# Two transformer blocks on one core: the second block's adaLN weight pieces loaded from the last gate projection to the seventh output block

## Chip, cores and metric

One core of one Trainium2 chip. The metric is device microseconds (us) of one execution of the program. The profiled execution is one of these; its span runs from the first to the last instruction of the program. Engines: PE multiplies matrices, DVE and ACT are the vector and scalar engines, POOL is GpSimd, SP issues nearly all loads.

## What is computed

A first block (retention and mLSTM mixer, then a gated feed-forward) and behind it a second block with two layers (attention mixers, each with an expert-choice feed-forward), on 256 tokens of width 1024. Cut to what the change touches:

```
# first block, end: output projection of the mixer, then the feed-forward (hidden width 2816)
x = x + g1 * mixer_output(...)
x = x + g2 * swiglu(modulate(rms_norm(x, norm2_gain[layer]), sh2, sc2), w_ffn_in[layer], w_ffn_out[layer])
# second block: six modulation vectors for each layer and each of two streams
m_lat = jnp.split((silu_c @ mod_w[layer] + mod_b[layer])[:, None, :], 6, axis=-1)
m_ctx = jnp.split((silu_cc @ mod_w[layer] + mod_b[layer])[:, None, :], 6, axis=-1)
h_lat = rms_norm_2(x_lat, norm1_g[layer]) * (1 + m_lat[1]) + m_lat[0]
```

All is in float32. The adaLN weights `mod_w` are 1024 x 6144 for each of two layers. They depend on nothing of the first block, so they can be multiplied whenever there is room.

## The kernel before

**Weights come as pieces through a ring.** Every weight matrix is cut into pieces of up to 2 MB (128 partitions x 4096 columns). `pieces` is one long list (lines 218 to 228) that says in which order they are loaded. Three buffers, R0, R1 and R2, take them in turn; other buffers (F, G, L, H, Y) join in where they are free. `Ring.done(slot)` says that a piece has been used; the next piece of the list is then loaded into that slot by a transfer that SP issues, and SP waits for the slot's last reader first. SP works through its instructions in order, so a transfer that waits holds those behind it.

**The names of the pieces.** `wout0` and `wout1` are the mixer's output projection, `fin0` to `fin10` the eleven column blocks of the feed-forward's first matrix, `fout0` to `fout7` the eight pieces of its second. The adaLN weights of the second block are 24 pieces, `moda0` to `moda11` (layer 0) and `modb0` to `modb11` (layer 1). In the trace and the order all tiles of the ring are called R, and the weights are `w_out`, `w_fin`, `w_fout`, `mod0` and `mod1`.

**How a weight block is multiplied.** `prod` takes cuts of 4 rows of 128 x 256 columns. Each cut is split into a high part (ACT, line 303) and the remainder (DVE, line 304), and each product is made of three matmuls (high x high, high x low, low x high). The splits go to three pairs of buffers (w4k twice, w4p once), so they run up to three cuts ahead of PE. A block `fin` is 4 cuts of 24 matmuls, 96 in all; a pair of `fout` pieces is 6 cuts and 132 matmuls. A ring slot is free as soon as its last cut is split.

**How an adaLN piece is multiplied.** Unsplit: `mod_group` (line 374) takes four pieces into one accumulator; each piece is 8 matmuls of 32x512, which the trace shows as 16 instructions on tile `aux`. After the fourth, ACT or DVE copies the sums out (`ev`), and four small matmuls (`aux<-cp,ev`, 8 instructions in the trace) put them in place. Six groups make the 24 pieces.

**What sets the place of a piece.** `aside` registers a generator, and `tick`, called after each job of `prod`, moves every generator one step. A step of `mod_group` is taken only if its piece is in the ring's list of loaded pieces. `need` ticks until a piece is there; `drain` ticks until the generators are done. So the code is written in an order that follows the list of pieces; a scheduler then orders each engine's instructions, and each engine runs them in that order.

```
    mods = [f"moda{i}" for i in range(12)] + [f"modb{i}" for i in range(12)]
    for i in range(11):
        seq(f"fin{i}", mods[3 + i])
    for i in range(8):
        seq(f"fout{i}", mods[14 + i])
    seq("evkv0", *mods[22:], "evin0", "evin1", "evin2", "evout0", "evout1")
```

Before, the list has one piece beside each `fin` and each `fout` block and the last two behind `evkv0`, the first weights of the second block. The groups are registered after the mixer's output projection (line 1037), between it and the norm that makes the feed-forward's input (`norm_sums`, L2 of the residual, then tile L).

Of the kernel before, what the change touches and what calls it, by code (L numbers as in the profile page):

```python
# [91 lines left out]
def body(ctx, tc, T, dbg=None, stop_at=None):  # L92
# [71 lines left out]
    def aside(*gens):  # L164
        g = chain(gens)
        beside.append(g)
        return g
# [5 lines left out]
    def after(g):  # L173
        while g in beside:
            yield
# [6 lines left out]
    def drain(upto=None):  # L182
        while beside and (upto is None or upto in beside):
            tick()
# [24 lines left out]
    def seq(*names):  # L209
        for n in names:  # L210
            base = n.rstrip("0123456789")
            src, cols = SRC[base]
            one(base, T[src], int(n[len(base):]), cols)
# [5 lines left out]
           "odukv": ("od_ukv", 2048), "oduq": ("od_uq", 2304), "odout": ("od_out", SLOT)}  # L219
    seq("ada0", "ada2", "win0", "ada1", "ada3", "win1", "ada4", "win2", "ada5", "win3", "ada6", "win4", "ada7",  # L220
        "win5", "ada8", "win6", "ada9", "win8", "win9", "win7", "win10", "ada10", "win11", "ada11", "up0", "up1",
        "wout0", "moda0", "wout1", "moda1", "moda2")
    mods = [f"moda{i}" for i in range(12)] + [f"modb{i}" for i in range(12)]
    for i in range(11):
        seq(f"fin{i}", mods[3 + i])
    for i in range(8):
        seq(f"fout{i}", mods[14 + i])
    seq("evkv0", *mods[22:], "evin0", "evin1", "evin2", "evout0", "evout1")

    def expert_pieces(layer):  # L230
        def add(e, *ws):
# [14 lines left out]
    ring = Ring(nc, slot, pieces)  # L246
# [6 lines left out]
    def S(name):  # L253
        a, b = off[name]
        return sm[:, a:b]
# [120 lines left out]
    def mod_group(names, bias, MOD):  # L376


        i0 = 4 * int(names[0][4:])
        ps = None  # L380
        for j, name in enumerate(names):
            while not ring.has(name):
                yield
            s_, W = ring.get(name)
            Wv = kv3(W)
            ps = aux() if ps is None else ps
            for k in range(2):
                for q in range(4):
                    mm(ps[32 * q:32 * q + 32, :], sT2[:, 2 * q + k, 6 - 2 * j:38 - 2 * j], Wv[:, 2 * q + k, :],
                       start=j == 0 and k == 0, stop=j == 3 and k == 1, tile_position=(0, 32 * q), skip_group_check=True)  # L390
            ring.done(s_)
            yield
        ev = work("ev", 512, 1)
        evac(ev, ps)
        yield
        p2 = aux()
        for c in range(4):
            mm(p2[:, 8 * c:8 * c + 8], ev[:, c * 128:c * 128 + 128], selm)
        dve.tensor_tensor(MOD[:, i0:i0 + 16, :].rearrange("p (i c) r -> p i c r", c=4),
                          p2[:, :32].rearrange("p (c i r) -> p i c r", c=4, i=4),  # L400
                          bias[:, i0:i0 + 16].rearrange("p (i c) -> p i c", c=4)[:, :, :, None].to_broadcast([P, 4, 4, 2]),
                          op=OP.add)

    def groups(*which):

        return aside(*[mod_group([f"mod{'ab'[g // 3]}{g % 3 * 4 + j}" for j in range(4)],
                                 S(f"mod_b{g // 3}"), (MOD20, MOD21)[g // 3]) for g in which])

    def need(name):

# [4 lines left out]
    def mod_steps0(name, sT, bias, MOD):  # L415

        i = int(name[4:] if name.startswith("mod") else name[3:])
        while not ring.has(name):
            yield
        s_, W = ring.get(name)  # L420
        Wv = kv3(W)
        ev = work("ev", 512, 1)
        for k in range(KC):
            sk = sT[:, k, 0:1]
            if k == 0:
                dve.tensor_scalar_mul(ev, Wv[:, k, :], sk)
            else:
                dve.scalar_tensor_tensor(ev, Wv[:, k, :], sk, ev, op0=OP.mult, op1=OP.add)
            if k % 2:
                yield  # L430
        ring.done(s_)
        p2 = aux()
        for c in range(4):
            mm(p2[:, c:c + 1], ev[:, c * 128:c * 128 + 128], ones[:, 0:1])
        dve.tensor_tensor(MOD[:, i * 4:i * 4 + 4, 0], p2[:, :4], bias[:, i * 4:i * 4 + 4], op=OP.add)
# [533 lines left out]
    for t in range(2):  # L969
        r = head_rstd(MLN[:, t, :], "hm", 512)  # L970
        m3 = MLN[:, t, :].rearrange("p (h c) -> p h c", h=4)
        dve.tensor_tensor(m3, m3, r[:, :4, None].to_broadcast([P, 4, 128]), op=OP.mult)
    aside(*[mod_steps0(f"ada{i}", sT1, S("b_ada"), MOD1) for i in (10, 11)])
    bg_proj(3, "win11")
    ring.add("L")
    ring.retire("L")
# [38 lines left out]

    def out_proj(name, X2, X, gate, post):
        for i in range(2):
            s_, W = ring.get(f"{name}{i}")
            for n2 in range(2):
                ps = acc()  # L1020
                prod([kv3(W)[:, :, n2 * 256:n2 * 256 + 256]], [col(ps[:, :N], 0, X2, True), col(ps[:, N:], 1, X2)])
                k = i * 4 + 2 * n2
                for j in range(2):
                    residual(X, k + j, ps[:, j * N:j * N + N], gate(k + j))
                post(X, k)
            ring.done(s_)

    drain()
    g1h = cst.tile([P, KC], F32, name="g1h")
    dve.tensor_scalar_mul(g1h, MOD1[:, 16:24, 0], 0.5)  # L1030
    add, read = sums()
# [2 lines left out]
    A2x = scale_vec("A2x", MOD1, 4, 0, S("norm2"))  # L1034
    H2 = slot("L")
    H2h, H2l = xv(H2), xv(H2[:, 2048:])
    groups_ = groups(*range(6))
    norm_sums(XLv, read, A2x, MOD1[:, 24:32, 0], H2h, H2l)
    close_phase()
    wk[2] = ctx.enter_context(tc.tile_pool(name="late", bufs=1))  # L1040
# [992 lines left out]
```

## Time and profile before

| | us |
|---|---|
| median of 3 runs | 1914.63 (1913.92 to 1922.8) |
| the profiled execution | 1914.88 |
| its span | 1913.0 |
| PE busy | 1662.7 (87%) |
| DVE busy | 738.2 (39%) |
| ACT busy | 529.0 (28%) |
| HBM read | 579.59 MB |

How to read it: the span holds stages with different bounds. Up to about 780 us the first block and the second block's first mixer are multiplied; from about 820 on the experts' weights stream in. An engine's busy share says little by itself; what counts is where PE or the loads wait, and for what. Engine rows of a timeline give start and length in us, and in brackets the idle time before them with what ended it. The clock column is the share of PE's full clock (2.4 GHz) that was granted; its low level is half (1.2 GHz).

### The profile page before, as it was taken

How to read it: one execution, taken by the hardware profiler on the slowest of the kernel's cores; microseconds unless marked ns; L12 is line 12 of the kernel's file. 1: busy time of each engine (PE TensorE's matmuls, PEld its weight loads, DVE VectorE, ACT ScalarE, POOL GpSimd, SP SyncE). 2: the span in 40 equal slices, each digit the busy share in tenths (PEclk: the TensorE clock that was granted, in tenths of full speed). 3: DMA queues.
4: the chain of work that ended last, by engine and by line, in shares of the span. 5: the costliest groups of instructions: out<-in, count | busy, mean ns of one | idle time of the engine just before them, and what ended most of it. 6: DMA issues, size and time to landing. Idle time of an engine off the chain costs nothing. (4 is left out here: it accounts for less than half of the span.)

```text
span 1913.0 us, 29571 instructions
## 1 busy us (share of the span) xinstructions
PE 1662.7 (87%) x12876; PEld 1153.6 (60%) x12876; DVE 738.2 (39%) x1430; ACT 529.0 (28%) x916; POOL 52.7 (3%) x51
## 2 busy tenths in 40 slices
PE   7999999999999998799999989889997666575655
PEld 3999997889887778744343423258686323242323
DVE  5956786444536645611211212145763110010101
ACT  3423554434435553311010100034542100010000
POOL 0100021000000000000000000001000000000000
PEclk8999999999999999899999999999998877897888
DMA  9445457877784111589999999953356999999997
GB/s 379 185 182 220 160 194 267 336 296 315 286 310 167 66 61 74 233 345 428 428 430 428 428 428 429 428 226 121 133 220 266 426 427 426 427 427 426 426 426 302
DMA packets 53985, 582.54 MB, mean 305 GB/s; under 512 B 5984, under 2 KB 5984, under 8 KB 20576
## 3 DMA queue, kind: packets, MB, share of 16 engines
q1 hardware_dynamic: 53136, 577.90, 74.0%
q10 hardware_dynamic: 720, 2.75, 0.4%
q8 instruction: 101, 1.65, 0.3%
q14 instruction: 28, 0.23, 0.0%
HBM read 579.59 MB, written 1.05 MB: 304 GB/s over the span
## 5 line engine op out<-in xcount | busy, mean ns | idle before, releaser
L187 PE MATMUL acc<-L,w4k 128*128 128x256 f32 (+3 forms) x1744 | 269.3, 328 | 12.6 <-DMA L<-w 9.5
L187 PE MATMUL acc<-H,w4k 128*128 128x256 f32 (+2 forms) x1608 | 246.2, 338 | 18.1 <-DMA H<-w 11.6
L187 PEld LDWEIGHTS acc<-L,w4k 128*128 128x128 f32 (+2 forms) x1744 | 207.1, 178 | 53.0 <-issue 32.4
L304 DVE TENSOR_TENSOR w4k<-R,w4k 128x1024 fp32r<-128x1024 f32 (+3 forms) x152 | 177.7, 1170 | 137.3 <-ACT w4k L303 133.2
L187 PEld LDWEIGHTS acc<-H,w4k 128*128 128x128 f32 (+2 forms) x1608 | 189.2, 178 | 56.4 <-issue 30.2
L303 ACT ACTIVATE w4k<-R 128x1024 fp32r<-128x1024 f32 (+3 forms) x152 | 154.2, 1016 | 213.3 <-PE acc L187 189.6
L187 PE MATMUL acc<-R,w4k 128*32 128x256 f32 (+1 forms) x1136 | 157.4, 513 | 45.6 <-DMA R<-w 45.6
L187 PEld LDWEIGHTS acc<-R,w4k 128*32 128x32 f32 (+1 forms) x1136 | 55.7, 132 | 131.9 <-issue 65.1
L199 DVE COPY t2k<-acc 128x512 f32<-128x512 f32 x24 | 16.6, 692 | 271.6 <-PE acc L187 271.5
L187 PE MATMUL aux<-R,t2k 128*32 128x256 f32 (+3 forms) x656 | 87.8, 512 | 20.7 <-DMA R<-w 20.3
L187 PE MATMUL acc<-G,w4k 128*32 128x256 f32 (+1 forms) x622 | 87.5, 408 | 20.6 <-DMA G<-w 20.6
L197 ACT ACTIVATE w4p<-aux 32x512 f32<-32x512 f32 (+1 forms) x58 | 28.1, 485 | 253.0 <-PE aux L187 185.3
L199 DVE COPY w4p<-aux 32x512 f32<-32x512 f32 (+1 forms) x58 | 32.5, 560 | 155.0 <-ACT w4p L197 108.9
L187 PE MATMUL acc<-F,w4k 128*32 128x256 f32 (+2 forms) x464 | 74.5, 450 | 8.3 <-DMA F<-w 8.3
L187 PEld LDWEIGHTS acc<-G,w4k 128*32 128x32 f32 (+1 forms) x622 | 57.8, 166 | 37.6 <-DMA G<-w 26.4
L304 DVE TENSOR_TENSOR w4p<-R,w4p 128x1024 fp32r<-128x1024 f32 x43 | 54.3, 1262 | 56.7 <-ACT w4p L303 56.5
L190 PE MATMUL tr<-cp,t2k 128*128 128x128 f32 (+1 forms) x290 | 45.7, 284 | 33.8 <-DVE t2k L199 12.0
L197 ACT ACTIVATE t2k<-acc 128x512 f32<-128x512 f32 x24 | 14.3, 597 | 217.3 <-PE acc L187 217.3
L190 PEld LDWEIGHTS tr<-cp,t2k 128*128 128x128 f32 (+1 forms) x290 | 31.7, 143 | 70.1 <-issue 25.1
L187 PEld LDWEIGHTS aux<-R,t2k 128*32 128x32 f32 (+1 forms) x656 | 33.4, 137 | 65.0 <-issue 34.3
L187 PE MATMUL acc<-Y,w4k 128*32 128x256 f32 (+1 forms) x464 | 56.7, 477 | 16.5 <-DMA Y<-w 16.5
L303 ACT ACTIVATE w4p<-R 128x1024 fp32r<-128x1024 f32 x43 | 45.6, 1060 | 75.3 <-PE acc L187 61.2
(460 smaller groups left out, 2537.8 us busy)
## 6 DMA issues: line engine op xcount, KB each, us to landing
R<-w SPq DMA_DIRECT2D x67, 2048.0 KB, 28.3
R<-mod SPq DMA_DIRECT2D x24, 2048.0 KB, 8.5
F<-w SPq DMA_DIRECT2D x23, 2048.0 KB, 29.4
H<-w SPq DMA_DIRECT2D x23, 2048.0 KB, 29.2
L<-w SPq DMA_DIRECT2D x23, 2048.0 KB, 26.2
Y<-w SPq DMA_DIRECT2D x23, 2048.0 KB, 27.5
R<-w_in SPq DMA_DIRECT2D x11, 2048.0 KB, 7.9
R<-w_fin SPq DMA_DIRECT2D x10, 2048.0 KB, 9.6
```

The costliest lines, as they stand in the source:

```text
L187: return pe.matmul(out, lhsT, rhs, start=start, stop=stop, **kw)
L190: return pe.transpose(out, in_, ident[:in_.shape[0], :in_.shape[0]])
L197: act.activation(out, in_, AF.Copy, scale=1.0 if scale is None else scale)
L199: dve.tensor_copy(out, in_)
L303: act.activation(rnd(hi), src, AF.Copy)
L304: dve.tensor_tensor(rnd(lo), src, hi, op=OP.subtract)
```

## The change

The list of pieces is dealt out anew and the groups are registered earlier. `moda0` to `moda3` come among `wout0`, `wout1` and `fin0`; behind each of `fin1` to `fin10` follow one or two pieces (two behind `fin2`, `fin5` and `fin8`), behind `fout0` to `fout6` one each, and none behind `fout7` and `evkv0`. The six groups are registered before the last gate projection (`win11`), to begin when the first block's own last adaLN pieces (`ada10`, `ada11`) are through. `out_proj` gets its weights by `need` in place of `ring.get`, and the `drain` ahead of it waits for `ada_` alone.

```
-        "wout0", "moda0", "wout1", "moda1", "moda2")
+        "moda0", "wout0", "moda1", "wout1", "moda2", "fin0", "moda3")
     mods = [f"moda{i}" for i in range(12)] + [f"modb{i}" for i in range(12)]
-    for i in range(11):
-        seq(f"fin{i}", mods[3 + i])
+    mods = mods[:3:-1]
+    for i in range(1, 11):
+        seq(f"fin{i}", *[mods.pop() for j in range(1 + (i % 3 == 2))])
     for i in range(8):
-        seq(f"fout{i}", mods[14 + i])
-    seq("evkv0", *mods[22:], "evin0", "evin1", "evin2", "evout0", "evout1")
+        seq(f"fout{i}", *[mods.pop() for j in range(min(len(mods), 1))])
+    seq("evkv0", "evin0", "evin1", "evin2", "evout0", "evout1")
...
-    def groups(*which):
+    def group(g):
 
-        return aside(*[mod_group([f"mod{'ab'[g // 3]}{g % 3 * 4 + j}" for j in range(4)],
-                                 S(f"mod_b{g // 3}"), (MOD20, MOD21)[g // 3]) for g in which])
+        return mod_group([f"mod{'ab'[g // 3]}{g % 3 * 4 + j}" for j in range(4)], S(f"mod_b{g // 3}"), (MOD20, MOD21)[g // 3])
...
-    aside(*[mod_steps0(f"ada{i}", sT1, S("b_ada"), MOD1) for i in (10, 11)])
+    ada_ = aside(*[mod_steps0(f"ada{i}", sT1, S("b_ada"), MOD1) for i in (10, 11)])
+    groups_ = aside(after(ada_), *[group(g) for g in range(6)])
     bg_proj(3, "win11")
...
-            s_, W = ring.get(f"{name}{i}")
+            s_, W = need(f"{name}{i}")
...
-    drain()
+    drain(ada_)
...
-    groups_ = groups(*range(6))
     norm_sums(XLv, read, A2x, MOD1[:, 24:32, 0], H2h, H2l)
```

What this does to the order, at three places. In the rows, R0 to R2 are the ring's slots with a running number, `w4k` and `w4p` the split weights, `acc` and `aux` accumulators; a wait on PE is one for matmuls, on DVE for a split or a sum, on Activation for ACT's, on DMAHW for a landing.

**First place: SP's transfers around fin3.** Before, from `moda4`'s (R0_11) to `fin4`'s (R2_13):

```order
L69 DMA R0_11_3538<-mod0 128x4096 [waits DMAHW7_49,DMAHW2_49,PE_49]
L69 DMA R1_11_3639<-mod0 128x4096 [waits DMAHW4_49,DMAHW5_49,DMAHW3_49,DVE_49]
L69 DMA R0_12_3585<-w_fin 128x4096 [waits DMAHW2_49,PE_49]
L69 DMA R2_12_3777<-mod0 128x4096 [waits DMAHW0_49,DVE_49]
L69 DMA R1_12_3667<-w_fin 128x4096 [waits DMAHW3_49,PE_49]
L69 DMA R0_13_3915<-mod0 128x4096 [waits DMAHW4_49,DVE_49]
L69 DMA R2_13_3805<-w_fin 128x4096 [waits DMAHW5_49,PE_49]
```

and of the change, from `moda5`'s (R2_12) to `fin5`'s (R0_13):

```order
L69 DMA R2_12_3639<-mod0 128x4096 [waits DMAHW6_49,DMAHW5_49,DMAHW7_49,DMAHW0_49,DVE_49]
L69 DMA R1_12_3787<-mod0 128x4096 [waits DMAHW1_49,DVE_49]
L69 DMA R2_13_3667<-mod0 128x4096 [waits DMAHW4_49,PE_49]
L69 DMA R0_12_3933<-mod0 128x4096 [waits DMAHW2_49,DVE_49]
L69 DMA R2_14_3689<-w_fin 128x4096 [waits DMAHW6_49,PE_49]
L69 DMA R1_13_3815<-w_fin 128x4096 [waits DMAHW5_49,PE_49]
L69 DMA R0_13_3962<-w_fin 128x4096 [waits DMAHW7_49,PE_49]
```

Before, each slot carries one piece between two blocks (`fin3`, R1_12, follows R1_11). Now slot R2 carries two pieces in a row, `moda5` (R2_12) and `moda6` (R2_13), before `fin3` (R2_14), whose transfer waits for the matmuls of `moda6`. The same stands ahead of `fin6` (`moda9`, `moda10`) and `fin9` (`modb1`, `modb2`).

PE of the change there, from `moda6` to the first matmuls of `fin3` (acc_50 and acc_51); between the row of acc_48 and that of `ev_14` are 19 more matmuls of `fin2`:

```order
L187 MATMUL aux_33_3520<-R2_13_3667,sT2_112 32x512 [waits DMAHW6_49]
L187 MATMUL aux_33_3520<-R2_13_3667,sT2_112 32x512 x7
L187 MATMUL aux_33_3520<-R1_12_3787,sT2_112 32x512 [waits DMAHW5_49]
L187 MATMUL aux_33_3520<-R1_12_3787,sT2_112 32x512 x7
L187 MATMUL acc_48_3789<-L_3_3443,w4p_51_3893 128x256
...
L187 MATMUL aux_34_3847<-cp_68,ev_14_3829 128x8 [waits DMAHW1_49,DMAHW0_49,DVE_49]
L187 MATMUL aux_34_3847<-cp_68,ev_14_3829 128x8 x3
L187 MATMUL aux_35_3953<-R0_12_3933,sT2_112 32x512 [waits DMAHW7_49,PE_49]
L187 MATMUL aux_35_3953<-R0_12_3933,sT2_112 32x512 x7
L187 MATMUL acc_50_3935<-L_3_3443,w4k_105_3937 128x256 [waits Activation_49]
L187 MATMUL acc_51_3936<-L_3_3443,w4k_105_3937 128x256 [waits DVE_49]
L187 MATMUL acc_50_3935<-L_3_3443,w4k_106_3938 128x256 [waits DVE_49]
```

Before, 145 matmuls of blocks and one more piece stand between the matmuls of R1_11 and the first of `fin3`; now it is `moda7`, 20 matmuls, the small group and `moda8`.

**Second place: PE between the output projection and fin0.** Before (`tr_29` are the norm's sums, `tr_30` its broadcast, acc_44 and acc_45 `fin0`):

```order
L187 MATMUL tr_29_3392<-ones_100,ss_3_3137 128x1 [waits DVE_49,PE_49]
L187 MATMUL aux_31_3450<-R0_9_3133,sT2_112 32x512 x6
L187 MATMUL aux_31_3450<-R2_10_3387,sT2_112 32x512 [waits DMAHW6_49]
L187 MATMUL aux_31_3450<-R2_10_3387,sT2_112 32x512 x7
L187 MATMUL tr_29_3392<-ones_100,t2k_86_3385 128x1 [waits Activation_49]
L187 MATMUL tr_30_3403<-cp_68,rs_r_7_3401 128x128 [waits PE_49,Pool_49]
L187 MATMUL acc_44_3464<-L_3_3391,w4k_89_3466 128x256 [waits Activation_49]
L187 MATMUL acc_45_3465<-L_3_3391,w4k_89_3466 128x256
L187 MATMUL aux_31_3450<-R0_10_3490,sT2_112 32x512 [waits DMAHW7_49]
L187 MATMUL aux_31_3450<-R0_10_3490,sT2_112 32x512 x7
L187 MATMUL acc_44_3464<-L_3_3391,w4k_89_3466 128x256 [waits DVE_49]
```

and of the change:

```order
L187 MATMUL tr_29_3444<-ones_100,ss_3_3146 128x1 [waits DVE_49]
L187 MATMUL aux_33_3520<-R0_10_3439,sT2_112 32x512 [waits DMAHW4_49,PE_49]
L187 MATMUL aux_33_3520<-R0_10_3439,sT2_112 32x512 x7
L187 MATMUL tr_29_3444<-ones_100,t2k_86_3437 128x1 [waits Activation_49]
L187 MATMUL tr_30_3455<-cp_68,rs_r_7_3453 128x128 [waits Pool_49]
L187 MATMUL acc_44_3502<-L_3_3443,w4k_89_3504 128x256 [waits Activation_49]
L187 MATMUL acc_45_3503<-L_3_3443,w4k_89_3504 128x256
L187 MATMUL acc_44_3502<-L_3_3443,w4k_89_3504 128x256 [waits DVE_49]
```

Nearly three pieces stood in the norm's way (`moda1`'s rest, `moda2`, `moda3`); now it is one, `moda4` (R0_10).

**Third place: SP's transfers around fout4.** Before, with `fout5` (R1_20) and `fout4` (R0_21):

```order
L69 DMA R0_20_5320<-mod1 128x4096 [waits DMAHW1_49,PE_49]
L69 DMA R2_20_5472<-mod1 128x4096 [waits DMAHW2_49,DVE_49]
L69 DMA R1_20_5474<-w_fout 128x2816 [waits DMAHW3_49,DVE_49]
L69 DMA R0_21_5342<-w_fout 128x2816 [waits DMAHW4_49,PE_49]
L69 DMA R2_21_5512<-mod1 128x4096 [waits DMAHW5_49,PE_49]
```

and of the change, with `fout5` (R2_24) and `fout4` (R0_20):

```order
L69 DMA R0_19_5350<-mod1 128x4096 [waits DMAHW4_49,PE_49]
L69 DMA R1_20_5511<-mod1 128x4096 [waits DMAHW5_49,DVE_49]
L69 DMA R2_24_5513<-w_fout 128x2816 [waits DMAHW6_49,DVE_49]
L69 DMA R0_20_5397<-w_fout 128x2816 [waits DMAHW7_49,PE_49]
L69 DMA R1_21_5551<-mod1 128x4096 [waits DMAHW0_49,PE_49]
```

`fout4` waits for a piece's matmuls as before. On PE, 37 matmuls and a piece stood between those matmuls and `fout4`'s first; now it is 55 and a piece (`modb9`, R1_20), and 38 matmuls later comes `modb10` (R1_21), loaded into the slot that `modb9` leaves.

## Rows read from the trace of the kernel before

**Rows 1.** Windows: busy us (instructions) of PE, PEld, DVE, ACT, POOL; clock, DMA share, GB/s.

```profile
270.00:322.00 52.00, 52.00 (x433) 49.08 (x431) 39.05 (x59) 24.79 (x32) 8.71 (x8) 1.00 0.73 275
322.00:339.00 17.00, 12.68 (x74) 5.58 (x73) 8.70 (x20) 5.61 (x11) 0.71 (x1) 0.81 0.79 318
339.00:530.00 191.00, 191.00 (x1597) 167.00 (x1599) 93.22 (x140) 79.28 (x115) 0.70 (x1) 1.00 0.78 308
530.00:541.00 11.00, 7.26 (x38) 6.33 (x31) 4.73 (x7) 4.84 (x7) 0.00 (x0) 0.69 0.85 308
...
573.00:596.00 23.00, 21.60 (x178) 16.54 (x177) 14.35 (x32) 10.35 (x18) 1.39 (x2) 1.00 0.67 270
596.00:780.00 184.00, 178.37 (x1366) 152.87 (x1365) 107.12 (x231) 96.59 (x183) 6.95 (x5) 0.98 0.19 67
825.00:1210.00 385.00, 363.42 (x1758) 146.87 (x1756) 69.31 (x128) 46.44 (x83) 0.00 (x0) 1.00 1.01 427
```

**Rows 2.** Timeline of PE, 318 to 345 us: start, length, instruction, count [idle before].

```profile
322.17 1.04 PE L187 MATMUL aux<-R,sT 128*32 128x512 f32 x2
...
323.45 3.63 PE L187 MATMUL aux<-R,sT 128*32 128x512 f32 x28
327.01 0.61 PE L187 MATMUL tr<-ones,t2k 128*128 128x1 f32 x4
...
329.33 0.71 PE L187 MATMUL tr<-cp,rs_r 128*128 128x128 f32 x4 [1.04 <-POOL rs_r L452]
331.15 0.50 PE L187 MATMUL acc<-L,w4k 128*128 128x256 f32 x2 [1.11 <-ACT L L480]
333.82 3.64 PE L187 MATMUL aux<-R,sT 128*32 128x512 f32 x16 [2.17 <-DMA R<-mod]
337.39 6.53 PE L187 MATMUL acc<-L,w4k 128*128 128x256 f32 x46
```

**Rows 3.** Timeline of PE, 526 to 545 us.

```profile
533.91 0.58 PE L187 MATMUL acc<-F,w4p 128*128 128x256 f32 x1 [3.28 <-ACT w4p L303]
...
535.17 0.80 PE L187 MATMUL acc<-F,w4p 128*128 128x256 f32 x2 [0.46 <-DVE w4p L304]
...
537.26 0.63 PE L187 MATMUL acc<-F,w4p 128*128 128x256 f32 x2
537.68 0.41 PE L187 MATMUL acc<-G,w4p 128*128 128x256 f32 x1
```

**Rows 4.** Timeline of ACT, 526 to 537 us.

```profile
532.80 1.06 ACT L303 ACTIVATE w4p<-R 128x1024 fp32r<-128x1024 f32 x1 [1.65 <-DMA R<-w_fout]
```

**Rows 5.** Timeline of PE, 397 to 415 and 427 to 449 us.

```profile
401.71 1.92 PE L187 MATMUL aux<-R,sT 128*32 128x512 f32 x16
403.57 3.24 PE L187 MATMUL acc<-L,w4k 128*128 128x256 f32 x25
...
441.03 0.95 PE L187 MATMUL aux<-cp,ev 128*128 128x8 f32 x8
441.84 5.88 PE L187 MATMUL acc<-L,w4k 128*128 128x256 f32 x48
447.56 1.56 PE L187 MATMUL acc<-L,w4p 128*128 128x256 f32 x12
```

**Rows 6.** Tile view of w_fin's loads issued at 411 and 403 us.

```profile
L69 SPq DMA_DIRECT2D R<-w_fin x1: 328/328/328, 411.4 to 411.4; - x1
DMA to landing us min/median/max: 7.6/7.6/7.6
...
L69 SPq DMA_DIRECT2D R<-w_fin x1: 328/328/328, 403.7 to 403.7; - x1
DMA to landing us min/median/max: 9.4/9.4/9.4
```

**Rows 7.** Tile view of w_fout's two loads issued from 520 to 525 us.

```profile
L69 SPq DMA_DIRECT2D R<-w_fout x2: 328/328/328, 520.7 to 524.3; - x2
...
DMA to landing us min/median/max: 7.9/8.1/8.4
```

**Rows 8.** Timeline of DVE, 320 to 340 us.

```profile
332.44 2.06 DVE L481 SCALAR_TENSOR_TENSOR L<-t2k,MOD,L 128x256 fp32r<-128x256 f32 x5
```

## Prediction

> **What bounds the kernel now.** I read the view by stretches first [rows 1]. From 270 to 322 and from 339 to 530 us PE is busy without a break (52.00 of 52, 191.00 of 191) at a granted clock of 1.00, while the loads take 0.73 and 0.78 of the DMA engines: PE is the bound there, and a load costs nothing as long as it lands in time. Two stretches stand out, 322 to 339 (12.68 of 17 busy, clock 0.81) and 530 to 541 (7.26 of 11, clock 0.69). From 596 to 780 PE is full again (178 of 184) with the queue almost idle (0.19). From 825 on the loads are the bound (share 1.01, 427 GB/s), and they can only start once the stage ahead has freed its buffers. So what is won or lost before 780 moves the end by the same amount.
>
> Next I read PE's timeline in the two holes. In the first [rows 2] the output projection ends at 322.2, and block fin0 gets going at 337.4. Between them stand 2 + 28 + 16 instructions of adaLN pieces (16 make one piece), and PE idles 1.04, 1.11 and 2.17 us, the last one for a piece's own load. In the second [rows 3] PE idles 3.28 us for ACT's split of an output block (L303) and 0.46 for DVE's. ACT's row [rows 4] says what that split itself waited for: the load, R<-w_fout. After both holes the clock is down: matmuls stand 0.21 us apart (two between 537.26 and 537.68) instead of 0.119 (48 between 441.84 and 447.56) [rows 3, 5].
>
> **The change part by part.** The sum is made against the profiled execution, 1914.88 us (span 1913.0), which is 0.25 over the median 1914.63. The number of pieces, their bytes and their matmuls stay: 24 pieces of 1.86 us on PE (401.71 to 403.57) and six small groups of 0.81 (441.03 to 441.84) [rows 5]. Where PE is full, a piece costs the same earlier or later, so the moves as such cost nothing; I count only where PE waits. One piece's worth of cover lost or gained is 1.86 us.
>
> *The feed-forward blocks.* Here the order shows a new dependence. Slot R2 used to carry one piece between two blocks; behind fin0, fin3 and fin6 it now carries two (moda5 and moda6; moda9 and moda10; modb1 and modb2). The load of fin3 waits for the matmuls of moda6, and on PE only this stands between moda6 and fin3's first matmul: moda7 1.86, 20 matmuls at 0.119 = 2.4, the small group 0.8, moda8 1.86, together 6.9 us. A block's load takes 7.6 us alone and 9.4 behind another one [rows 6]; moda8's load is ahead of it but nearly done (it goes out when fin2's last split is made, some 5 us before), so I take 7.9. Landing isn't enough: in the second hole the load landed at 524.3 + 8.4 = 532.7 [rows 7], ACT began at 532.80 [rows 4], PE's first matmul came at 533.91 and the first that needs DVE's low part at 535.17 [rows 3], 2.5 us after the landing. Four matmuls of the new order need the high part alone, which gives 0.5 back. So PE waits 7.9 + 2.5 - 0.5 - 6.9 = **3.0 us, three times: 9.0**. Bounds: 8.1 (landing in 7.6) to 13.5 (in 9.4); a gain is excluded, since the load can't go out before its slot is free. The other blocks' loads go out some 15 us or more ahead of their use, and cost nothing unless they queue behind a late one; fin4 and fin5 do, but fin4 has a whole block (96 matmuls, 11.4 us) more. The Trainium skill (DMA: Bandwidth & Descriptors, section Anatomy of one DMA) fits a transfer of GpSimd's queue as 2.0 us plus the bytes over 436 GB/s, an estimate of 6.8 us for these 2 MB; the row has 7.6 and decides, and by the page each wait would be 0.8 shorter and the sum 2.4 lower.
>
> *The clock after these waits.* Idling of 3.7 us (second hole) and 4.3 (first) was followed by the low level of 1.2 GHz. 1.4 us of idling in small bits between 573 and 596 was not (clock 1.00) [rows 1 to 3]. The price is 11 x 0.31 = 3.4 us in the second hole, of which some 0.3 fell into idling: 3.1. A wait of 3.0 (in two pieces, about 2 and 1) lies nearer the 3.7 than the 1.4. I take a fall after two of the three: **6.2**, with bounds 0 and 9.3.
>
> *The first hole.* The whole first group (moda0 to moda3) now runs before it, and one piece (moda4) inside it. Today 15.2 us less 46/16 pieces (5.3) is 9.9 us of hole proper. After the change: from the sums over t2k (327.01) to the first low half of fin0's input (DVE, 332.44 + 0.41) the chain takes 5.8 us [rows 2, 8], and the piece ahead of it covers the rest but for 0.3 to 1.3 us (fin0's load now goes out behind moda4's, some 15 us later than before, and its splits stand ahead of the last t2k on ACT): 6.1 to 7.1, so 3.3 won. The clock gives most of it back: now the low level lasts only 1 to 2 us beyond 337.4, while afterwards it would run against full work for up to 3.1. Taken **-1.0**; bounds 0 and -4 (no fall).
>
> *The output blocks.* The late load here is fout4 before and after, and again it waits for a piece's matmuls. 37 matmuls and a piece covered it; now 55 and a piece do, 6.6 + 1.9 = 8.5 us against 8.4 + 2.5 - 0.2, leaving 2.2 instead of 3.7. Then piece modb10 reuses the slot that modb9 has just left (7.9 us) with 2.2 + 4.3 us of cover: 1.3 more. Without a fall of the clock that is 3.5 against today's 3.7 + 3.1, with one it is about even: taken **-2.0**, bounds +0.5 and -3.3.
>
> *The tail of the feed-forward.* Three pieces leave the stretch 573 to 596 and the next stage's weights load that much sooner; the idling there is 23.00 - 21.60 = 1.4 us [rows 1]. Taken **-1.0**, bounds 0 and -1.4. Behind it the mixer's order shifts by a few matmuls with the same work: nothing, +-1.
>
> Sum: 9.0 + 6.2 - 1.0 - 2.0 - 1.0 = +11.2, so **1926 us**.
>
> **The rivals.**
> *Every wait pays for the clock.* All three block waits, and the one at fout4, are followed by the low level. For it: both long holes of today were. Against: those idled longer. 11.2 + 3.1 + 2.5 = +16.8, 1932 us; with the three blocks alone 1929. The Trainium skill (TensorE: Matmul & The Clock Gate, section HAM oscillation — how this bites in real kernels) speaks for it and against this change: a loop that waits for a load at each tile starts each tile at the throttled clock. By that rule the time is 1929; the trace agrees for idling of 3.7 and 4.3 us, and no row shows one of 3.0.
> *The waits come, the clock hardly falls.* With the waits cut in two by the matmuls that need the high part alone, the clock holds at the blocks, and at the first hole too: 9.0 - 4.0 - 3.3 - 1.0 = +0.7, 1915.6; with one or two falls anywhere 1919 to 1921.
> *Not slower: the block loads are in time and the two old holes close.* The place is slot R2 behind moda6, moda10 and modb2; it decides itself at a landing 4.9 us after those matmuls (6.9 - 2.5 + 0.5). Then -4.0 - 3.3 - 1.0 = -8.3, 1906.6, and 1903 if fout4 were in time too. For it: the queue has a fifth of its time free. Against: no 2 MB load of the rows landed in less than 7.6 us [rows 6], and the wait on the piece's matmuls stands in the order.
>
> **How the numbers follow.** 0.5% (9.6 us) is about what a measurement of this kernel can tell from no change, so slower begins at 1924.2 and faster at 1905.1. The forecast, two falls and 1922 to 1928, has a chance of 0.38; every wait paying (1928 to 1934) 0.20; few falls (1915 to 1922) 0.29; loads in time (1903 to 1910) 0.09; something unseen, 0.04, half of it faster. Slower: four fifths of the forecast and all of the first rival, 0.50. Faster: 0.05 of the third and 0.02, 0.07. Within: 0.43. The range 1916 to 1932 leaves out the third rival, the upper end of the first and the lower end of the second, together about 0.2; of the forecast alone it is 1922 to 1928.
>
> **What would show it.** In the changed profile PE's waits between 330 and 490 us should show three of about 2 us on ACT's split (L303) and three of about 1 us on DVE's (L304), each ACT split waiting for R<-w_fin; the loads of fin3, fin6 and fin9 issued some 7 us before their block; the clock below 1.00 after at least two of them; the hole after the output projection with one piece in it, about 9 us long; and fout4's wait under 3 us. If PE is full from 339 to 480 as it is now, the central step is wrong. If the three waits are there and the time is near 1916, the clock term was mis-sized; if it is over 1932, some load I counted as early is late too.

## The result and the profile after

The changed kernel takes 1933.08 us (median of five, 1929.98 to 1936.05) against 1914.63: a ratio of 1.0082, interval 1.0067 to 1.0098, so it is slower by 0.8%. The two medians lie 18.45 us apart; by the ratio and its interval the change costs 15.7 us (12.8 to 18.8), a time of about 1930. The direction and the place were forecast, the size was too small: 11.4 us. The median is 1.1 us above the range's upper end of 1932, the time by the ratio lies inside the range. The profiled execution has 1933.08 us too, and a span of 1931.3 against 1913.0.

The view by stretches of the changed kernel (stretch, its length, busy us and instructions of PE, PEld, DVE, ACT, POOL; clock, DMA share, GB/s), cut so that each place stands alone:

```profile
328.00:345.00 17.00, 12.35 (x81) 10.26 (x81) 12.19 (x27) 8.16 (x13) 1.66 (x1) 0.80 0.82 343
345.00:380.00 35.00, 35.00 (x299) 30.67 (x299) 14.37 (x20) 13.21 (x19) 0.00 (x0) 1.00 0.69 260
380.00:395.00 15.00, 10.24 (x62) 8.42 (x61) 5.64 (x8) 4.81 (x6) 0.00 (x0) 0.77 0.90 375
395.00:430.00 35.00, 35.00 (x298) 30.66 (x297) 13.49 (x18) 12.22 (x18) 0.00 (x0) 1.00 0.68 257
430.00:443.00 13.00, 8.70 (x60) 6.97 (x59) 5.32 (x11) 4.88 (x7) 0.00 (x0) 0.87 0.99 410
443.00:480.00 37.00, 37.00 (x319) 32.65 (x321) 15.68 (x21) 12.78 (x20) 0.00 (x0) 1.00 0.71 271
480.00:493.00 13.00, 8.93 (x64) 7.22 (x64) 5.65 (x9) 4.43 (x5) 0.00 (x0) 0.87 0.82 344
...
550.00:570.00 20.00, 16.42 (x114) 12.91 (x113) 6.82 (x10) 5.70 (x8) 0.00 (x0) 0.83 0.86 313
570.00:596.00 26.00, 25.99 (x220) 24.22 (x219) 11.90 (x17) 8.71 (x12) 0.00 (x0) 1.00 0.69 260
...
612.00:795.00 183.00, 178.81 (x1354) 153.03 (x1353) 111.22 (x238) 95.69 (x187) 6.43 (x5) 0.98 0.19 66
```

The 191 us between the two holes, full before [rows 1], now have three breaks, 49 us apart: PE idles 15 - 10.24 = 4.76, 13 - 8.70 = 4.30 and 13 - 8.93 = 4.07 us, and the clock is down in each. The DMA engines are not the bound over the whole: their share is 0.68 to 0.71 ahead of and between the breaks, and 0.82 to 0.99 in them. Only single loads come too late.

PE's timeline of the changed kernel at fin3, fin6 and fin9 (start, length, instruction, count, idle before and what ended it; the split is line 304 on ACT and 305 on DVE here, one more than before):

```profile
380.75 1.93 PE L187 MATMUL aux<-R,sT 128*32 128x512 f32 x16
387.40 8.85 PE L187 MATMUL acc<-L,w4k 128*128 128x256 f32 x46 [4.73 <-ACT w4k L304]
...
436.95 0.73 PE L187 MATMUL acc<-L,w4k 128*128 128x256 f32 x4 [3.78 <-ACT w4k L304]
438.21 6.99 PE L187 MATMUL acc<-L,w4k 128*128 128x256 f32 x44 [0.53 <-DVE w4k L305]
...
485.41 0.73 PE L187 MATMUL acc<-L,w4k 128*128 128x256 f32 x4 [3.54 <-ACT w4k L304]
486.67 6.72 PE L187 MATMUL acc<-L,w4k 128*128 128x256 f32 x44 [0.53 <-DVE w4k L305]
```

ACT's timeline there says what its split waited for, the landing:

```profile
386.29 1.06 ACT L304 ACTIVATE w4k<-R 128x1024 fp32r<-128x1024 f32 x1 [4.88 <-DMA R<-w_fin]
...
435.85 1.06 ACT L304 ACTIVATE w4k<-R 128x1024 fp32r<-128x1024 f32 x1 [3.93 <-DMA R<-w_fin]
```

And the tile view of the loads of w_fin and of mod (issue time, then us to landing): moda8 issued at 371.1, fin3 at 375.8, fin4 at 377.5, and fin6 and fin9 at 426.3 and 475.0.

```profile
L69 SPq DMA_DIRECT2D R<-mod x1: 328/328/328, 371.1 to 371.1; - x1
DMA to landing us min/median/max: 8.7/8.7/8.7
L69 SPq DMA_DIRECT2D R<-w_fin x1: 327/327/327, 375.8 to 375.8; - x1
DMA to landing us min/median/max: 10.5/10.5/10.5
L69 SPq DMA_DIRECT2D R<-w_fin x1: 328/328/328, 377.5 to 377.5; - x1
DMA to landing us min/median/max: 13.6/13.6/13.6
...
L69 SPq DMA_DIRECT2D R<-w_fin x1: 328/328/328, 426.3 to 426.3; - x1
DMA to landing us min/median/max: 9.5/9.5/9.5
...
L69 SPq DMA_DIRECT2D R<-w_fin x1: 328/328/328, 475.0 to 475.0; - x1
DMA to landing us min/median/max: 9.3/9.3/9.3
```

moda8 lands at 371.1 + 8.7 = 379.8, four us after fin3's load has gone out, and fin4's goes out 1.7 behind it. Ahead of fin6 and fin9 the piece's load has 2.9 and 3.2 us to go (issued at 421.6 and 470.3, landing 7.6 and 7.9 later). So the load that PE waits for shares the queue on both sides.

The hole after the output projection, PE's timeline of the changed kernel:

```profile
329.01 1.92 PE L187 MATMUL aux<-R,sT 128*32 128x512 f32 x16
331.46 0.61 PE L187 MATMUL tr<-ones,t2k 128*128 128x1 f32 x4 [0.52 <-ACT t2k L496]
...
334.73 0.71 PE L187 MATMUL tr<-cp,rs_r 128*128 128x128 f32 x4 [1.99 <-POOL rs_r L452]
336.55 0.79 PE L187 MATMUL acc<-L,w4k 128*128 128x256 f32 x2 [1.11 <-ACT L L480]
338.36 6.85 PE L187 MATMUL acc<-L,w4k 128*128 128x256 f32 x39 [1.02 <-DVE L L481]
```

One piece stands in it, as the order said, and the wait for a piece's load (2.17 us) is gone [rows 2]. But PE idles 4.65 us (17 - 12.35) where it idled 4.32: without the other pieces the norm's own chain (ACT's square, GpSimd's root, ACT's and DVE's halves of the input) shows in full. And the low clock, which fell on a piece inside the hole before (3.64 us for its 16 instructions in place of 1.86), now falls on fin0's matmuls, 39 in 6.85 us, 2.2 more than at 0.119 each.

The balance, against [rows 1], with the clock's loss taken as the window's length times the missing share, less what fell into idling: blocks 13.1 of idling and 6.4 of clock; first hole +0.3; fout4 3.58 against 3.74 of idling and the same clock, -0.2; the tail of the feed-forward 0.3 (a single wait just behind 612) against 1.4, -1.1; the mixer behind it 3.9 (4.2 less that 0.3) against 5.6, -1.7. That is 16.8. The chain of work ahead of the experts stands here, PE's timeline of the changed kernel:

```profile
820.75 0.58 PE L190 MATMUL tr<-cp,aff 128*16 128x128 f32 x2 [2.79 <-DVE aff L1161]
```

The same instruction stood at 805.09 before, so 15.7 of the 18.3 us of span are lost by then. The other 2.6 appear in the stretch bound by loads, where two executions of one kernel differ by about as much (second batch below): I can name no cause for them, nor for the 1.1 us between the balance and this row.

### The profile page after: what moved, and what is told of

It reads as the page before. It is cut to its first block, busy times and chain, and to the rows that moved or that the text cites. A ratio compares the mean times of both kernels' runs of the same rounds, so it can differ in the third digit from the quotient of the medians.

```text
span 1931.3 us, 29546 instructions
## 1 busy us (share of the span) xinstructions
PE 1667.5 (86%) x12876; PEld 1161.3 (60%) x12876; DVE 738.2 (38%) x1430; ACT 525.7 (27%) x914; POOL 54.5 (3%) x51
## 5 line engine op out<-in xcount | busy, mean ns | idle before, releaser
L187 PE MATMUL acc<-L,w4k 128*128 128x256 f32 (+3 forms) x1744 | 274.7, 331 | 26.6 <-ACT w4k L304 12.0
L187 PEld LDWEIGHTS acc<-L,w4k 128*128 128x128 f32 (+2 forms) x1744 | 212.7, 183 | 63.7 <-issue 24.3
L305 DVE TENSOR_TENSOR w4k<-R,w4k 128x1024 fp32r<-128x1024 f32 (+3 forms) x155 | 182.5, 1178 | 145.2 <-ACT w4k L304 144.0
L187 PE MATMUL acc<-L,w4p 128*128 128x256 f32 x416 | 66.7, 281 | 0.0
```

Source lines behind the costliest of these rows:

```text
L187: return pe.matmul(out, lhsT, rhs, start=start, stop=stop, **kw)
L305: dve.tensor_tensor(rnd(lo), src, hi, op=OP.subtract)
```

## Experiments

Every kernel was timed beside the kernel before on one chip; a batch shares these runs, in which the kernel before had medians of 1917.07, 1915.80, 1916.19 and 1917.57 us in the four batches. So the ratio says more than the time, and the expected times of the first batch, set against 1914.63, are to be read 2.4 us higher. "Idle at fin" is PE's waiting for splits between 345 and 500 us, "idle at fout4" that ahead of the third output pair, both from the profile.

| | us | ratio to before | idle at fin | idle at fout4 |
|---|---|---|---|---|
| before | 1914.63 | | 0 | 3.74 |
| changed | 1933.08 | 1.0082 (1.0067 to 1.0098) | 13.1 | 3.58 |
| one piece beside each block | 1916.30 | 0.9994 (0.9984 to 1.0005) | 0 | 3.88 |
| pairs alone | 1929.46 | 1.0064 (1.0050 to 1.0078) | 13.2 | 3.91 |
| before, fout4 and fout5 exchanged | 1918.08 | 1.0010 (1.0001 to 1.0018) | 0 | 2.27 |
| changed, three loads halved | 1916.29 | 0.9994 (0.9984 to 1.0003) | 5.3 | 3.76 |
| changed again | 1932.50 | 1.0088 (1.0075 to 1.0102) | 13.8 | 3.83 |
| changed, fin halved, fout4 in three | 1913.26 | 0.9985 (0.9973 to 0.9996) | 4.0 | 2.28 |
| before, fout4 in three | 1915.56 | 0.9998 (0.9989 to 1.0007) | 0 | 2.28 |
| changed, all cut | 1912.47 | 0.9983 (0.9974 to 0.9992) | 4.4 | 2.28 |
| before, all cut | 1916.26 | 0.9991 (0.9978 to 1.0004) | 0 | 2.29 |
| one each, all cut | 1912.55 | 0.9977 (0.9967 to 0.9988) | 0 | 2.29 |
| changed, all cut, once more | 1912.71 | 0.9982 (0.9971 to 0.9993) | 4.0 | 2.28 |
| the same, fout4 and fout5 exchanged, squares on GpSimd | 1913.62 | 0.9978 (0.9967 to 0.9989) | 3.7 | 0 |

### First batch: which part of the change costs, and what PE waits for

**One piece beside each block**, the early registration kept:

```
-        seq(f"fin{i}", *[mods.pop() for j in range(1 + (i % 3 == 2))])
+        seq(f"fin{i}", mods.pop())
...
-        seq(f"fout{i}", *[mods.pop() for j in range(min(len(mods), 1))])
-    seq("evkv0", "evin0", "evin1", "evin2", "evout0", "evout1")
+        seq(f"fout{i}", mods.pop())
+    seq("evkv0", *mods[::-1], "evin0", "evin1", "evin2", "evout0", "evout1")
```

> The changed kernel with its early registration and its first group ahead of fin0 kept, but one piece beside each fin and fout block and the last two behind evkv0, as before. Theory A (the three pairs of pieces in one slot cost the time: 13.1 us of waits and 6.4 of clock): PE waits for no split between 345 and 500 us, clock 1.00 there, the hole after the output projection stays as in the changed kernel (idle 4.6), fout4's wait as before: 1913 to 1917 us. Rival B (the early registration and the first group's place cost a part): PE still loses time ahead of or behind the blocks and the time is above 1919.

Measured: 1916.30, no difference from before. In its view by stretches PE is full where the changed kernel breaks three times:

```profile
345.00:500.00 155.00, 155.00 (x1307) 137.74 (x1306) 76.34 (x106) 66.31 (x95) 0.70 (x1) 1.00 0.76 298
```

**The pairs alone**: the kernel before with its registration and first pieces, and the changed kernel's distribution from fin0 on.

```
-    for i in range(11):
-        seq(f"fin{i}", mods[3 + i])
-    for i in range(8):
-        seq(f"fout{i}", mods[14 + i])
-    seq("evkv0", *mods[22:], "evin0", "evin1", "evin2", "evout0", "evout1")
+    mods = mods[:2:-1]
+    for i in range(11):
+        seq(f"fin{i}", *[mods.pop() for j in range(1 + (i % 3 == 2))])
+    for i in range(8):
+        seq(f"fout{i}", *[mods.pop() for j in range(min(len(mods), 1))])
+    seq("evkv0", "evin0", "evin1", "evin2", "evout0", "evout1")
```

> The complement: the kernel before, with its registration behind the output projection and its first four pieces where they were, and only the pairs (behind fin2, fin5 and fin8, none behind fout7 and evkv0). Theory A: three waits of 4 to 5 us ahead of fin3, fin6 and fin9, each followed by the low clock, 1930 to 1935 us. Rival B: clearly less, 1920 to 1927, since only a part comes from the pairs.

Measured: 1929.46, 0.6% slower, half a us below the expected interval. The view of waits on PE, 340 to 500 us:

```profile
PE acc L187 <- ACT w4k L304: 12.7, 3, 5.2
PE acc L187 <- DVE w4k L305: 0.5, 1, 0.5
```

Three waits, 13.2 us, as in the changed kernel. The two kernels together settle the main question: the pairs cost what the change costs, and the earlier registration with its first group costs nothing by itself. Between pairs alone (1.0064) and the changed kernel (1.0082, 1.0088 when repeated) 3 to 5 us remain; the intervals just overlap, and this stays open.

**fout4 and fout5 exchanged** in the kernel before, for the old wait there:

```
-        seq(f"fout{i}", mods[14 + i])
+        seq(f"fout{(0, 1, 2, 3, 5, 4, 6, 7)[i]}", mods[14 + i])
```

> The kernel before, with fout4 and fout5 exchanged in the list of pieces alone. The one long wait of the output blocks comes because fout5's load, needed 66 matmuls later, is issued 3.6 us ahead of fout4's. Theory C (the order of these two loads is the cause): fout4 lands some 4 us sooner, the wait of 3.28 and 0.46 us and the low clock behind it (loss 3.1) go: 1907 to 1910 us. Rival D (the wait is for the slot that a piece's matmuls hold, whichever block is loaded there, and moves to fout5 or to the next pieces): 1912 to 1916 us.

Measured: 1918.08, 0.1% slower. The wait at fout4 fell to 1.52 and 0.75 us, but it did not go, although its load landed at 520.0 + 8.0 = 528.0; a second wait came at fout6 (0.97, 0.17 and 0.76 us between 555 and 558). PE's idling in the tail (0.73 and 0.58 us) is as long as before. Theory C gave the size of half the effect. Of rival D the wait that moves came true; the time, 1.0 us above the 1917.07 of this batch, is near the upper end of what D stands for against 1914.63 (-2.6 to +1.4). ACT's timeline of this kernel shows why the first wait stayed:

```profile
528.95 0.63 ACT L496 ACTIVATE t2k<-XL 128x512 f32<-128x512 f32 x1 [10.02 <-DVE XL L563]
529.49 0.89 ACT L499 ACTIVATE t2k<-XL,sm 128x256 f32<-128x256 f32 x2
530.28 1.04 ACT L303 ACTIVATE w4p<-R 128x1024 fp32r<-128x1024 f32 x1
```

fout4's split (the last row) no longer waits for a landing. It stands on ACT behind the squares of the residual (L496, L499), which wait for DVE's residual (L563), and that for PE's last matmul of the pair before. In the kernel before, these squares end at 531.16, and the landing let the split begin at 532.80 [rows 4]: the late load hid them.

**The three loads halved** in the changed kernel:

```
-                step = 1024 if cut or name in CUT else n
+                step = 1024 if cut or name in CUT else 2048 if name in ("fin3", "fin6", "fin9") else n
```

> The changed kernel with the loads of fin3, fin6 and fin9 issued in two halves. The first split reads the first half alone. Theory A with PE waiting for the landing of the block: each of the waits (4.73, 4.31, 4.07 us) shortens by 2 to 2.5 us, and the clock falls after fewer of them: 1919 to 1927 us. Rival E (the halves share the queue with moda8 ahead and fin4 behind, so that the first half lands hardly sooner): 1930 to 1934 us.

Measured: 1916.29, no difference from before, and better than theory A expected. PE's timeline of this kernel at fin3, and its view by stretches at fin3, fin6 and fin9:

```profile
385.15 0.74 PE L187 MATMUL acc<-L,w4k 128*128 128x256 f32 x4 [1.95 <-ACT w4k L304]
386.41 5.50 PE L187 MATMUL acc<-L,w4k 128*128 128x256 f32 x44 [0.52 <-DVE w4k L305]
```

```profile
378.00:395.00 17.00, 14.53 (x120) 12.80 (x121) 8.52 (x11) 7.17 (x10) 0.00 (x0) 1.00 0.99 398
...
425.00:440.00 15.00, 13.77 (x117) 12.04 (x116) 8.41 (x14) 7.47 (x9) 0.00 (x0) 1.00 1.02 421
...
470.00:483.00 13.00, 11.41 (x97) 9.68 (x96) 7.62 (x11) 6.00 (x7) 0.00 (x0) 1.00 1.02 418
```

The waits are down from 13.1 to 5.3 us (2.47 + 1.23 + 1.59), and the clock does not fall at all: 7.8 and 6.4, together 14.2 of the 16.8 us by which the time fell. So PE waited for the landing of a whole block of which the first split reads a quarter (128x1024 of 128x4096), and the clock's part of the price is real: it goes when the waits are short. A half does not land in half the time: fin3's first half took 7.7 us to land where the whole took 10.5, with moda8's load still in flight ahead of it and its own second half 0.4 us behind. Cutting into quarters was not tried.

### Second batch: the changed kernel repeated, and the last wait

**The changed kernel again**, unaltered.

> The changed kernel once more, unaltered, so that it and its variants are timed on one chip. Theory A: three waits ahead of fin3, fin6 and fin9 as in its first profile, 1930 to 1936 us, so that the halved loads (1916.29) gave back some 16 us, the waits' 13.1 less the 5.3 that stayed and the 6.4 of clock. Rival F (the chip and the day make up the difference between it and the kernel with only the pairs, 1929.46): 1927 to 1930.

Measured: 1932.50, ratio 1.0088, as before (waits 12.7 and 1.1 us at the blocks). Its span is 1933.1 with the experts' first wait at 820.27; the first profile had 1931.3 with 820.75. So the part bound by loads alone differs by 2.3 us between two executions of one kernel, and by 2.6 between the two of the changed kernel with all cuts below (spans of 1908.6 and 1910.0 us, that wait's end at 801.14 and 799.92), which is why I give no cause for the 2.6 us above.

**fout4's load cut in three**, in the changed kernel with the halves, and in the kernel before alone:

```
-                step = 1024 if cut or name in CUT else n
+                step = 1024 if cut or name in CUT else {"fin3": 2048, "fin6": 2048, "fin9": 2048, "fout4": 1024}.get(name, n)
...
-                    self.nc.sync.dma_start(t[:, i:i + step], src[:, i:i + step])
+                    self.nc.sync.dma_start(t[:, i:min(i + step, n)], src[:, i:min(i + step, n)])
```

> The changed kernel with the loads of fin3, fin6 and fin9 in two halves and fout4's in three parts. If the wait at fout4 (3.17 and 0.59 us and the low clock behind it, 2.9 to 3.1) is one for the landing of its whole load, it shortens by some 2 us and the clock stays: 1910 to 1913 us, under the kernel before. If not, because fout5's load shares the queue: 1914 to 1917.

> The kernel before with fout4's load in three parts alone. The same two readings: 1910 to 1913 if PE waits there for the whole landing, 1914 to 1917 if the first part lands hardly sooner or the wait moves to the next pieces as it did when fout4 and fout5 were exchanged.

Measured: 1913.26, ratio 0.9985 (0.9973 to 0.9996), the first kernel here below before, by 0.15%; and 1915.56, no difference (0.9998), in which the chain ahead of the experts is 3.6 us earlier (801.53) and the end only 1.0. In both the wait fell from 3.7 to 1.52 and 0.76 us, so PE had waited there for the whole landing. The time shows little of it: the first kernel's interval overlaps that of the three halved loads alone (0.9984 to 1.0003). A part of the rest is again ACT's order, as in the exchange; ACT's timeline of the first of the two:

```profile
539.61 0.63 ACT L496 ACTIVATE t2k<-XL 128x512 f32<-128x512 f32 x1 [10.03 <-DVE XL L563]
540.15 0.89 ACT L499 ACTIVATE t2k<-XL,sm 128x256 f32<-128x256 f32 x2
540.94 1.04 ACT L304 ACTIVATE w4p<-R 128x1024 fp32r<-128x1024 f32 x1
```

fout4's first part landed at 532.0 + 8.2 = 540.2 here, and the split began 0.7 us later, behind the squares; in the second kernel it landed at 523.6 + 5.5 = 529.1, and the split began at 530.40. So ACT's order holds the split up by 0.7 and 1.3 us; the rest of the 2.28 is not put down to it.

**All blocks cut**: fin1 to fin10 in halves, all fout in three.

> The changed kernel with the loads of fin1 to fin10 in halves and of all fout blocks in three parts. If only the loads that are late matter, it is within 1.5 us of the kernel with those four cut; if more and smaller transfers slow the queue, the adaLN pieces land later and it is 2 to 5 us slower than that.

Measured: 1912.47, ratio 0.9983 (0.9974 to 0.9992), 0.8 us from the kernel with four loads cut. Only the late loads matter, and smaller transfers cost nothing that shows.

### Third batch: what the cuts and the distribution give apart

> The kernel before with the loads of fin1 to fin10 in halves and of all fout blocks in three parts. If the new distribution of the pieces gains something by itself once its late loads are mended, this kernel stays above the changed one with the same cuts (1912.47): 1914 to 1916 us. If the cuts alone make the gain, it is there too: 1911 to 1913.

> The changed kernel with one piece beside each block, two behind evkv0, and the same cuts. Against the cut changed kernel it has no pair, so no wait at the fin blocks (3 to 4 us there now), but more pieces at the tail, where PE idled 2.1 us instead of 0.3: 1910 to 1913 us if both terms count as in the profiles; 1914 to 1916 if the early registration brings nothing.

> The changed kernel with all cuts once more, for the comparison with the other two on one chip: 1911 to 1914 us.

Measured: 1916.26 (0.9991, interval 0.9978 to 1.0004), 1912.55 (0.9977, 0.9967 to 0.9988) and 1912.71 (0.9982, 0.9971 to 0.9993). With the cuts, both kernels with the early registration are faster than before, and the kernel before with the same cuts is not clear of no change. The medians of the three say that the early registration gives some 3.6 us, but the intervals overlap, so this is likely and not shown. Between pairs and one piece each there is no difference any more, although PE still waits 4.0 us at the blocks of the one and not at all at those of the other; what makes up for that I did not trace.

### Fourth batch: the squares on GpSimd

The changed kernel with all cuts, fout4 ahead of fout5, and the squares behind the second output pair taken from ACT:

```
+            if pool:
+                v = sq.rearrange("p (c n) -> p c n", c=2)
+                if scale is None:
+                    pool_e.tensor_tensor(v, X[:, k:k + 2, :], X[:, k:k + 2, :], op=OP.mult)
+                else:
+                    pool_e.tensor_tensor(v, X[:, k:k + 2, :], scale[:, k:k + 2, None].to_broadcast([P, 2, N]), op=OP.mult)
+                    pool_e.tensor_tensor(v, v, v, op=OP.mult)
...
-        add1(XLv, 2 * n4)
-        add2(XLv, 2 * n4, fg)
+        add1(XLv, 2 * n4, pool=n4 == 1)
+        add2(XLv, 2 * n4, fg, pool=n4 == 1)
```

> The changed kernel with all cuts, fout4's load ahead of fout5's, and the squares that follow the second output pair computed on GpSimd in place of ACT. With the cuts PE still waits 1.52 and 0.76 us at fout4, and ACT starts that split right behind three squares that waited for DVE's residual, not at the landing. Theory G (the rest of that wait is ACT's order): the wait falls under 0.5 us, no low clock there, 1908.5 to 1911 us against 1912.5 and 1912.7. Rival H (the wait moves to fout6, as in the exchange of fout4 and fout5, or GpSimd's work slows DVE): 1912 to 1915.

Measured: 1913.62, ratio 0.9978 (0.9967 to 0.9989), no better than the 0.9983 without. ACT's and then PE's timeline of this kernel:

```profile
537.87 1.06 ACT L304 ACTIVATE w4p<-R 128x1024 fp32r<-128x1024 f32 x1 [6.73 <-DMA R<-w_fout]
```

```profile
540.08 1.92 PE L187 MATMUL aux<-R,sT 128*32 128x512 f32 x16
541.94 0.38 PE L187 MATMUL acc<-F,w4p 128*128 128x256 f32 x1
...
562.39 1.06 PE L187 MATMUL aux<-cp,ev 128*128 128x8 f32 x8 [0.84 <-DVE ev L199]
...
565.08 0.50 PE L187 MATMUL acc<-F,w4p 128*128 128x256 f32 x2 [1.06 <-DVE w4p L305]
```

Theory G holds at its place: the split follows the landing at once (532.2 + 5.6 = 537.8), and PE goes from the piece into fout4 without a gap. The exchange is part of this run and brought the landing forward too (533.9 + 6.4 = 540.3 with all cuts alone), so what the squares give by themselves is not separated. Rival H holds for the time: 1.9 us of waits come up at fout6 instead. Its second half is seen as well, DVE's two splits beside GpSimd's squares took 2.93 us in place of 2.09, but GpSimd is idle again from 546 us on and the waits come at 562 and 565; which half makes them is open. So the wait at this place can be removed, and by itself that gains no time.

## Why the prediction was right and wrong

**The pairs.** Right, and shown from both sides (one piece each: no waits and no loss; pairs alone: 13.2 us of waits). The dependence read in the order, slot R2's second piece ahead of fin3, fin6 and fin9, is where the time went, and where the loads go out 11.6 (387.4 - 375.8), 10.6 and 10.4 us ahead of their block's first matmul: a cover of 6.9 and the wait.

**The size of the waits.** This is the step that failed: "moda8's load is ahead of it but nearly done, so I take 7.9". Three waits of 3.0 were forecast; they are 4.73, 4.31 and 4.07. The loads took 10.5, 9.5 and 9.3 us, moda8's had 4.0 us to go and not almost none, and fin4's, which I had put down as harmless, went out 1.7 us behind. The forecast's own numbers said as much: a load that takes 7.6 us and went out some 5 us earlier has 2.6 to go. Put into the forecast's own sum (landing + 2.5 - 0.5 - 6.9) these landings give 5.6, 4.6 and 4.4, within 0.3 to 0.9 of the waits, so the working of the sum was right and one term was mis-sized. The total, 13.1, is near the upper bound given, 13.5, which stood for the row with 9.4 us "behind another load". That row was the nearer one: its load went out at 403.7, when a piece's load (399.5 + 7.9) had 3.7 us to go. And the row of 7.6, which I had read as a load alone, went out at 411.4, when the one before it (403.7 + 9.4) had 1.7 us to go. The kernel before has a third load of a block, which went out when a piece's load (426.2 + 7.9) had 3.9 us to go, with nothing behind it for 8 us; the tile view of w_fin at 430 us:

```profile
L69 SPq DMA_DIRECT2D R<-w_fin x1: 328/328/328, 430.2 to 430.2; - x1
DMA to landing us min/median/max: 10.9/10.9/10.9
```

So with 1.7 us to go for the load ahead a block's load took 7.6, with 2.9 to 3.2 it took 9.3 to 9.5, and with 3.7 to 4.0 it took 9.4 to 10.9. That the load behind, fin4's, lengthens it as well is not shown. The Trainium skill's fit of a single transfer on GpSimd's queue (DMA: Bandwidth & Descriptors, section Anatomy of one DMA), by which these 2 MB would take an estimated 6.8 us, is farther off than the row of 7.6: it has no term for the neighbours in the queue, and the measurement decides. Put in for the 7.9 of the sum it would have shortened each wait by 1.1 us, not by the 0.8 stated.

**The clock.** 6.2 forecast for two full falls; 6.4 measured from a large one after the 4.73 us wait (0.77 over 15 us) and two half as large (0.87 over 13 us). So the first rival, a fall after every wait, was right in number, and the forecast in sum, by luck: three falls of different sizes came to what two equal ones would have. That the rival's 1932 lies nearest to the median is luck as well: its clock at the blocks, 9.3, was 2.9 too high and its waits, 9.0, were 4.1 too low. The Trainium skill's rule (TensorE: Matmul & The Clock Gate, section HAM oscillation — how this bites in real kernels), that a loop waiting for a load at each tile starts each at the throttled clock, is borne out for waits of 4.1 to 4.7 us by these three clocks of 0.77, 0.87 and 0.87 only in part: fin3 starts at the low level, while at fin6 and fin9 the first four matmuls still take 0.73 us (0.74 in the halved kernel at a clock of 1.00) and the level falls behind them. With the waits cut to 1.2 to 2.5 us, in the halved kernel, the clock was 1.00.

**The first hole.** -1.0 forecast, about +0.3 measured. The hole proper did shrink, but the 3.3 us counted as won were no idling: the chain's own waits (0.52, 1.99, 1.11 and 1.02 us) leave as much of it as before, and the clock's loss moved from a piece to fin0, as the forecast had it.

**The output blocks.** -2.0 forecast, -0.2 measured. The wait for modb10 did not come, but fout4's stayed, 3.12 and 0.46 us in place of the 2.2 forecast. It is the same mis-sized term: its load took 10.4 us, 1.4 behind fout5's, where 8.4 was taken.

**The tail and the rest.** -1.0 forecast, -1.1 measured; the mixer -1.7, which was put down as nothing, +-1.

So of the 7.1 us by which the sum (11.2) fell short of the span's 18.3, 4.1 are the landings at the blocks, 1.3 the first hole, 1.8 the output blocks and 0.2 the clock; the tail and the mixer take 1.8 back, and 1.5 is unexplained (2.6 behind 821, less 1.1 ahead of it). The rival of loads in time fell; what decided it was the landing, as stated, at 9.3 to 10.5 us where 4.9 were needed. The sign for a time over 1932, that some load counted as early is late too, pointed the wrong way: from 345 to 550 us PE waits for no block but fin3, fin6 and fin9.

## What to carry to other kernels

When a ring slot takes one transfer more before a block, look at the queue at the moment the block's load can go out: count how long the transfer ahead still has to go (its issue time plus a row's duration), and take the row of a load that went out behind as much, not the shortest one. Where a consumer needs only part of a block at first, cutting the late load is the cheap cure: here it gave back nearly the whole loss, 16.8 us, waits and clock, without a change in the order of the work. And a late load can hide a second wait on the engine that reads it; look at what stands ahead of the reader on its own engine before you count the whole wait as won.

## Unexpected

The changed kernel with all cuts was profiled twice, and PE idled 2.28 us at fout4 in both (33 - 30.72). The clock stayed in one and fell in the other. The view by stretches of the first and of the second:

```profile
527.00:560.00 33.00, 30.72 (x256) 25.75 (x256) 11.30 (x15) 8.39 (x11) 0.00 (x0) 1.00 0.92 360
```

```profile
527.00:560.00 33.00, 30.72 (x244) 25.74 (x243) 10.70 (x14) 7.87 (x10) 0.00 (x0) 0.95 0.89 339
```

And a wait of 1.95 and 0.52 us ahead of fin3 (the three halved loads) left it at 1.00, while one of 2.02 and 0.51 at the same place (the first execution with all cuts) did not: the 44 matmuls behind it took 5.50 us in the one and 7.00 in the other. So at this size the same wait in the same program is or isn't followed by the low level; the forecast's question, whether 3 us lie nearer to 3.7 or to 1.4, had no fixed answer in this range. The level also falls where PE does not wait at all. The same two executions with all cuts, from 565 to 600 us, again the first and the second:

```profile
565.00:600.00 35.00, 35.00 (x287) 34.62 (x285) 20.73 (x39) 15.87 (x24) 1.39 (x2) 0.95 0.39 147
```

```profile
565.00:600.00 35.00, 35.00 (x297) 34.30 (x296) 22.17 (x41) 17.02 (x26) 1.39 (x2) 1.00 0.40 150
```

PE is busy throughout. Before the fall it ran matmuls of one column (`tr<-ones`, 128x1) for 2.4 us, from 583.4 to 585.7, and in the second execution just as long; the 32 matmuls of a block behind them took 5.53 us in the first and 4.01 in the second. So a count of PE's waits does not give every fall. What decides it these runs do not show.
